# A two-layer float32 streaming-encoder trunk: reordered first feed-forward products, a kept transpose, and squared ReLU two tiles at a time

## The chip, the core and the metric

The kernel runs on one core of one Trainium2 chip. The metric is the device time of one execution in microseconds (us); a kernel's time is the median of several executions.

## What is computed

The input is x of 256 frames by 2048 features (batch 1), float32 throughout. The reference, cut to its skeleton:

```python
# layer 1 ("mixer A")
u = rms_norm(h, a_norm_g);  q, k, v, fz = split(u @ a_w_in)      # 16 heads of 128
q = rms_norm(q) ; k = rms_norm(k)                                # per head
logf = log_sigmoid(fz + a_b_f)
o = softmax(q k^T / sqrt(128) + c_q - c_k, causal) v             # c = cumsum(logf)
h = h + o @ a_w_out
h = h + sq_relu_mlp(h, mlp_norm_g[0], mlp_w1[0], mlp_w2[0])
# keys and values for layer 2, once
k_sh, v_sh = split(rms_norm(h, kv_norm_g) @ kv_w);  k_sh = rms_norm(k_sh)
# layer 2 ("mixer B")
q = rms_norm(rms_norm(h, b_norm_g) @ b_w_q)
o = chunked attention of q against k_sh, v_sh with a relative-position bias
h = h + o @ b_w_out
h = h + sq_relu_mlp(h, mlp_norm_g[1], mlp_w1[1], mlp_w2[1])

def sq_relu_mlp(h, g, w1, w2):          # w1: 2048 x 8192, w2: 8192 x 2048
    a = relu(rms_norm(h, g) @ w1)
    return (a * a) @ w2
```

## The kernel before, in words

**Precision by splitting.** A float32 number is held as a high part in TensorE's float32r type and a low part, the rest. A weight unit (128 partitions x 1024 numbers, 512 KB) is brought by one DMA into `raw` (4 buffers), cast to `hi` on ACT (L99), and `lo = raw - hi` is formed on DVE (L100); `hi` and `lo` have 3 buffers each. `fetch()` keeps two units ready ahead of the one in use. Activations are split in the same way: an activation tile `act` has the high part of 256 frames in its first 256 columns and the low part in the other 256. Of the four cross products only high x high, high x low and low x high are computed.

**Two kinds of panel.** `panel_a` has the activations as stationary operand and streams 512 weight columns: for each of 16 input tiles and 2 blocks of frames it issues three 512-column products (L222, L223, L224). A panel is 96 products over 8 weight units. `panel_b`, used for the first feed-forward product alone, has the weights as stationary operand and streams the activations, so that its output is already transposed for the second product. It makes two output tiles of 128 features at a time; for each of 16 input tiles and each output tile it issues one product of the high weights with both halves of x (512 columns, L238) and one of the low weights with the high half (256 columns, L239). A unit holds 4 input tiles, so 8 such pairs, and a panel has 4 units.

**The feed-forward block** (`mlp`) runs over four chunks of 2048 hidden features. A chunk is 8 `panel_b` panels, whose outputs go through `act` (sum of the two halves, squared ReLU, split: ACT L447 and L452, DVE L448, L450 and L453), and then four `panel_a` panels that multiply the chunk by its part of the second weight matrix and add to the residual `h` (L269, L271). The residual is kept with frames on the partitions.

**Turning the residual.** The next product needs the residual transposed. After each of a block's last panels, `next_x` puts two calls of `turn_x` into `fill`, a list of small jobs; `run_fill` takes one entry after each weight unit. `turn_x` transposes two feature tiles (four transposes of 128x128 on TensorE, L132) into the single PSUM buffer of the pool `ps_t`, and `split_x` reads them out with the gain (ACT L123, DVE L124). The same buffer serves `turn`, which transposes normed heads (`qn`, L254) for queries and keys (L261, read by ACT L262), and a few others. The head norm in front of it goes ACT (L246), DVE (L248, L250), POOL (L252), DVE (L254).

After layer 1's feed-forward block the residual is transposed twice: once with the gain of layer 2's queries (`xb`, from `next_x`), and once more for the shared keys and values (`xkv`), with the order of frames reversed inside each block of 128. The second set of 8 `turn_x` calls is put into `fill` and runs during the four panels of the queries (about 1130 to 1230 us), one call every second unit.

**Buffers and order.** PSUM accumulators come from `ps_acc`, 4 buffers of one bank, and activation tiles from `acts`, 32 buffers. The framework that compiles the kernel sets all waits and may move instructions of one engine past each other, by its own reckoning of when their inputs and buffers are there; what it has set is then fixed, and every engine runs its list in order.

Of the kernel before, what the change touches and what calls it, by code (L numbers as in the profile page):

```python
# [21 lines left out]
GH = 4  # L22
# [8 lines left out]
UB = UN // 256  # L31
# [4 lines left out]
def trunk(ctx: ExitStack, tc: tile.TileContext, xT, xr, gs, hg, bf, wgate, w_in, w_oa, w1a, w2a,  # L36
          w_kv, w_qb, w_ob, w1b, w2b, rel, out):
    nc = tc.nc
    V, S, G, TE = nc.vector, nc.scalar, nc.gpsimd, nc.tensor

    def pool(name, bufs, **kw):
        return ctx.enter_context(tc.tile_pool(name=name, bufs=bufs, **kw))

    PSUM = bass.MemoryType.PSUM
    wsp = pool("wsp", 3)
    acts = pool("acts", 32)
    wraw = pool("wraw", 4)
# [11 lines left out]
    h = [const.tile([P, D], F32, name=f"h{b}") for b in range(NB)]  # L59
# [23 lines left out]
    for srcs in ((w_in,), (w_oa,), (w1a, w2a), (w_qb,), (w_kv,), (w_ob,), (w1b, w2b)):  # L83
        n = srcs[0].shape[0] // (NCH if len(srcs) > 1 else 1)
# [25 lines left out]
    def run_fill():  # L110
        if fill:
            for f in fill.popleft():
                f()

    def blocks(t, flipped=False):
        t = t.rearrange("p (b t) -> p b t", b=NB)
        return t[:, :, ::-1] if flipped else t

    def split_x(src, m, which, flipped=False):
        g = gsb[:, which * KT + m : which * KT + m + 1]  # L120
        x = acts.tile([P, 2 * T], F32R, name="act")
        src = blocks(src, flipped)
        S.activation(blocks(x[:, :T]), src, AF.Copy, scale=g)  # L123
        V.scalar_tensor_tensor(blocks(x[:, T:]), src, g, blocks(x[:, :T].bitcast(F32)), op0=ALU.mult, op1=ALU.subtract)  # L124
        return x

    def turn_x(k0, which, into, flipped=False):
        pt = ps_t.tile([P, 512], F32, name="pt")
        for j in range(2):
            for b in range(NB):  # L130
                c = (k0 + j) * P
                TE.transpose(pt[:, j * T + b * P : j * T + (b + 1) * P], h[b][:, c : c + P], ident)  # L132
        for j in range(2):
            into.append(split_x(pt[:, j * T : (j + 1) * T], k0 + j, which, flipped))

    class ColumnStats:
        def __init__(self):
# [70 lines left out]
            self.flipped = f  # L208

    def panel_a(x, evac, before=None):  # L210
        ps = [ps_acc.tile([P, 512], F32, name="acc") for _ in range(NB)]
        for u in range(KT // UA):
            if before:
                before(u)
            hi, lo = fetch(min(u, AHEAD) if before else AHEAD)
            for j in range(UA):
                k = u * UA + j
                wh, wl = hi[:, j * 512 : (j + 1) * 512], lo[:, j * 512 : (j + 1) * 512]
                for b in range(NB):
                    xh = x[k][:, b * P : (b + 1) * P]  # L220
                    xl = x[k][:, T + b * P : T + (b + 1) * P]
                    TE.matmul(ps[b], xh, wh, start=k == 0, stop=False)  # L222
                    TE.matmul(ps[b], xh, wl, start=False, stop=False)  # L223
                    TE.matmul(ps[b], xl, wh, start=False, stop=k == KT - 1)  # L224
            run_fill()
        for b in range(NB):
            evac(b, ps[b])

    def panel_b(x, evac, n):
        for m in range(n):  # L230
            ps = [ps_acc.tile([P, 512], F32, name="acc") for _ in range(2)]
            for u in range(KT // UB):
                hi, lo = fetch()
                for i in range(2):
                    for j in range(UB):
                        k = u * UB + j
                        c = j * 256 + i * P
                        TE.matmul(ps[i], hi[:, c : c + P], x[k], start=k == 0, stop=False)  # L238
                        TE.matmul(ps[i][:, :T], lo[:, c : c + P], x[k][:, :T], start=False, stop=k == KT - 1)  # L239
                run_fill()  # L240
            for i in range(2):
                evac(2 * m + i, ps[i])

    def head_norm(ps, e, gcol, dst, b):
        sq = wk.tile([P, 512], F32, name="sq", tag="wk")
# [28 lines left out]
    def next_x(n, r2, stats, which, into):  # L274
        add_h = residual(n, r2)

        def f(b, ps):
            add_h(b, ps)
            stats.add(b, n)
            if b == NB - 1:  # L280
                add_fill([[lambda j=j: turn_x(4 * n + 2 * j, which, into)] for j in range(2)])
        return f

    def softmax(st, g, a, q, k, bias, cq):
# [28 lines left out]
    def values(st, a, v, o, i):  # L313
        po = ps_o.tile([P, 512], F32, name="po")
        TE.matmul(po[:, :T], v[:, 0, a * P : (a + 1) * P], st["pT"][:, :T], start=True, stop=False)  # L315
        TE.matmul(po[:, P:T], v[:, 1, a * P : (a + 1) * P], st["pT"][:, T:], start=False, stop=True)  # L316
        o[i] = acts.tile([P, 2 * T], F32R, name="act")
# [27 lines left out]
    x = []  # L345
# [80 lines left out]
    o = [None] * H  # L426
    for g in range(NG):
        q, k, v = qkv.tile([P, GH, T], F32, name="q", bufs=4), qkv_tile("k"), qkv.tile([P, NB, 512], F32, name="v")
# [12 lines left out]
    def mlp(x, st, last):  # L441
        for c in range(NCH):
            hid = []

            def act(m, ps):
                tb = wk.tile([P, T], F32, name="tb", tag="wk")
                S.activation(tb, ps[:, T:], AF.Copy)  # L447
                V.tensor_tensor(tb, ps[:, :T], tb, op=ALU.add)  # L448
                a = wk.tile([P, T], F32, name="a", tag="wk")
                V.scalar_tensor_tensor(a, tb, 0.0, tb, op0=ALU.max, op1=ALU.mult)  # L450
                t = acts.tile([P, 2 * T], F32R, name="act")
                S.activation(t[:, :T], a, AF.Copy)  # L452
                V.tensor_tensor(t[:, T:], a, t[:, :T].bitcast(F32), op=ALU.subtract)  # L453
                hid.append(t)

            panel_b(x, act, 8)
# [8 lines left out]
    mlp(x1, st1, lambda n, r2: next_x(n, r2, st2, 3, xb))  # L465
# [19 lines left out]
    o = [None] * H  # L485
    for g in range(NG):
        k, v = qkv_tile("k"), qkv.tile([P, NB, 512], F32, name="v")
# [80 lines left out]
```

## Time and profile before

| | |
|---|---|
| median of 3 runs | 2231.23 us (2229.55 to 2231.32) |
| the profiled execution, its own time | 2231.47 us |
| its span | 2229.7 us |
| TensorE (PE) | busy 2216.1 us, 99% |
| weight loads (PEld) | busy 1860.5 us, 83% |
| VectorE (DVE) / ScalarE (ACT) | 1294.5 us (58%) / 1053.5 us (47%) |
| DMA | 416.24 MB, mean 187 GB/s |
| 512-column product, `panel_a` (L222, L223, L224) | 2048 each; 397, 390, 390 ns |
| 512-column product, `panel_b` (L238) | 2048; 397 ns |
| 256-column product, `panel_b` (L239) | 2048; 281 ns |
| transposes in `turn_x` (L132) | 128; 275 ns |

Times in a row of the profile are the recorded duration of one instruction. Products on TensorE are pipelined, so that one starts before the recorded end of the one ahead; what a product costs in a stream is the distance from its start to the next start. In a timeline row the first number is the start from the beginning of the span, the second the duration (both in us), then engine, line, operation, output tile, input tiles and shape; in square brackets stands the idle time before it and what ended it. A row of a table of stretches gives the stretch, its length, the busy time and number of instructions of PE, PEld, DVE, ACT and POOL, the granted TensorE clock (1.00 is full), the DMA share and GB/s.

### The profile page before, as it was taken

What the parts mean: (1) busy time and instruction counts of PE and PEld (TensorE: products, weight loads), DVE (VectorE), ACT (ScalarE), POOL (GpSimd) and SP (SyncE); (2) the same over time, 40 slices, a digit from 0 to 9 for tenths busy, and PEclk for the clock granted to TensorE, in tenths of its full rate; (3) what the DMA queues carried; (4) which work ended last, traced back from release to release, by engine and by line L of the source; (5) the groups of instructions that cost most, each with busy time, mean ns of one, the idle gap of its engine ahead of it and who ended that gap; (6) DMA issues with size and microseconds to landing.
All of it is one profiled execution on the core that took longest, in us unless ns stands there. A gap on an engine that the chain in (4) does not pass through costs nothing.

```text
span 2229.7 us, 28337 instructions
## 1 busy us (share of the span) xinstructions
PE 2216.1 (99%) x10894; PEld 1860.5 (83%) x10894; DVE 1294.5 (58%) x1726; ACT 1053.5 (47%) x1451; POOL 41.6 (2%) x48
## 2 busy tenths in 40 slices
PE   9999999999999999999999999999999999999999
PEld 7788888888888888888887888888888888888887
DVE  6665555665565565565555655656655655655654
ACT  5554555543444444344455555555434444443443
POOL 1000000000000000000001000000000000000000
PEclk9999999999999999999999999999999999999999
DMA  7655556566656666666555655556666666666665
GB/s 260 201 173 173 183 175 186 183 190 194 192 184 194 189 189 189 193 186 189 181 181 163 184 176 163 166 183 185 189 193 190 188 191 192 187 192 193 187 200 162
DMA packets 117943, 416.24 MB, mean 187 GB/s; under 512 B 13216, under 2 KB 17456, under 8 KB 117552
## 3 DMA queue, kind: packets, MB, share of 16 engines
q1 hardware_dynamic: 117808, 414.44, 60.2%
q8 instruction: 85, 1.39, 0.3%
q14 instruction: 50, 0.41, 0.0%
HBM read 412.26 MB, written 2.12 MB: 186 GB/s over the span
## 4 chain that ended last, share of the span: by engine, by line
PE 96%; DMA 1%; DVE 1%; issue 0%; POOL 0%; ACT 0%; SPq 0%; DVEq 0%; ACTq 0%; POOLq 0%
PE acc L238 21%; PE acc L224 20%; PE acc L222 20%; PE acc L223 20%; PE acc L239 11%; DMA raw<-in_w_in 1%; PE pt L132 1%; PE pt L261 1%; PE po L315 1%; PE s L287 1%; DMA bias<-cd 1%; PE pt L309 0%; POOL rn L252 0%; DVE lo L100 0%; PE po L316 0%
## 5 line engine op out<-in xcount | busy, mean ns | idle before, releaser
L100 DVE TENSOR_TENSOR lo<-raw,hi 128x1024 fp32r<-128x1024 f32 (+1 forms) x770 | 938.9, 1221 | 809.9 <-ACT hi L99 809.7
L99 ACT ACTIVATE hi<-raw 128x1024 fp32r<-128x1024 f32 (+1 forms) x770 | 815.0, 1058 | 1054.3 <-PE acc L224 623.9
L222 PE MATMUL acc<-hi,act 128*128 128x512 f32 x2048 | 812.6, 397 | 2.1 <-ACT act L123 1.3
L224 PE MATMUL acc<-hi,act 128*128 128x512 f32 x2048 | 798.8, 390 | 0.5 <-DVE act L124 0.5
L223 PE MATMUL acc<-lo,act 128*128 128x512 f32 x2048 | 798.4, 390 | 0.1
L238 PE MATMUL acc<-act,hi 128*128 128x512 f32 x2048 | 721.1, 397 | 0.0
L239 PE MATMUL acc<-act,lo 128*128 128x256 f32 x2048 | 574.9, 281 | 0.0
L238 PEld LDWEIGHTS acc<-act,hi 128*128 128x128 f32 x2048 | 384.4, 188 | 93.0
L224 PEld LDWEIGHTS acc<-hi,act 128*128 128x128 f32 x2048 | 384.6, 188 | 83.0 <-DVE act L124 1.6
L222 PEld LDWEIGHTS acc<-hi,act 128*128 128x128 f32 x2048 | 384.9, 188 | 79.6 <-ACT act L123 2.0
L223 PEld LDWEIGHTS acc<-lo,act 128*128 128x128 f32 x2048 | 385.2, 188 | 77.8 <-DVE lo L100 1.6
L239 PEld LDWEIGHTS acc<-act,lo 128*128 128x128 f32 x2048 | 386.9, 189 | 0.3
L447 ACT ACTIVATE tb<-acc 128x256 f32<-128x256 f32 x128 | 47.9, 374 | 26.9 <-PE acc L239 26.9
L450 DVE SCALAR_TENSOR_TENSOR a<-tb 128x256 f32<-128x256 f32 x128 | 54.4, 425 | 4.4
L453 DVE TENSOR_TENSOR act<-a,act 128x256 fp32r<-128x256 f32 x128 | 53.5, 418 | 0.0
L448 DVE TENSOR_TENSOR tb<-acc,tb 128x256 f32<-128x256 f32 x128 | 53.4, 417 | 0.0
L452 ACT ACTIVATE act<-a 128x256 fp32r<-128x256 f32 x128 | 51.2, 400 | 0.0
L123 ACT ACTIVATE act<-pt,gsb 128x256 fp32r<-128x256 f32 x64 | 30.0, 469 | 38.0 <-DVE act L124 33.6
L252 POOL TENSOR_TENSOR rn<-vv,mhalf 128x4 f32<-128x4 f32 x32 | 36.0, 1125 | 407.0 <-DVE vv L250 407.0
L254 DVE TENSOR_TENSOR qn<-acc,rn 128x512 f32<-128x512 f32 x32 | 22.1, 691 | 35.7 <-POOL rn L252 35.7
L124 DVE SCALAR_TENSOR_TENSOR act<-pt,gsb,act 128x256 fp32r<-128x256 f32 x64 | 30.7, 480 | 16.7 <-ACT act L123 16.7
L300 ACT ACTIVATE pr<-t,nm 128x128 f32<-128x128 f32 x64 | 28.7, 449 | 14.8 <-DVE nm L299 14.4
(107 smaller groups left out, 551.0 us busy)
## 6 DMA issues: line engine op xcount, KB each, us to landing
raw<-in_w1a SPq DMA_DIRECT2D x128, 512.0 KB, 3.8
raw<-in_w2a SPq DMA_DIRECT2D x128, 512.0 KB, 3.7
raw<-in_w1b SPq DMA_DIRECT2D x128, 512.0 KB, 4.2
raw<-in_w2b SPq DMA_DIRECT2D x128, 512.0 KB, 4.3
raw<-in_w_in SPq DMA_DIRECT2D x94, 512.0 KB, 3.9
raw<-in_w_kv SPq DMA_DIRECT2D x64, 512.0 KB, 3.6
raw<-in_w_oa SPq DMA_DIRECT2D x32, 512.0 KB, 3.6
raw<-in_w_qb SPq DMA_DIRECT2D x32, 512.0 KB, 3.6
```

Of the source, the lines that this page charges most:

```text
L99: S.activation(hi[:, c], raw[:, c], AF.Copy)
L100: V.tensor_tensor(lo[:, c], raw[:, c], hi[:, c].bitcast(F32), op=ALU.subtract)
L222: TE.matmul(ps[b], xh, wh, start=k == 0, stop=False)
L223: TE.matmul(ps[b], xh, wl, start=False, stop=False)
L224: TE.matmul(ps[b], xl, wh, start=False, stop=k == KT - 1)
L238: TE.matmul(ps[i], hi[:, c : c + P], x[k], start=k == 0, stop=False)
L239: TE.matmul(ps[i][:, :T], lo[:, c : c + P], x[k][:, :T], start=False, stop=k == KT - 1)
L447: S.activation(tb, ps[:, T:], AF.Copy)
L448: V.tensor_tensor(tb, ps[:, :T], tb, op=ALU.add)
L450: V.scalar_tensor_tensor(a, tb, 0.0, tb, op0=ALU.max, op1=ALU.mult)
L452: S.activation(t[:, :T], a, AF.Copy)
L453: V.tensor_tensor(t[:, T:], a, t[:, :T].bitcast(F32), op=ALU.subtract)
```

## The change

1. *Order of the first products.* `panel_b` takes a function that lists the 16 products of a weight unit as (part, q): part 0 is the 512-column product, part 1 the 256-column one, and q = 0..7 counts output tile and input tile. The orders, with W for a 512-column product and N for a 256-column one: `pairs` WN WN ..., as before; `later` NW NW ..., except that in a panel's first unit each output tile begins with its W; `split` WW NN WW NN ...; `mirror` WN NW WN NW ...; `grouped` eight W, then eight N. Layer 1's four chunks use: pairs; later; grouped in the chunk's first unit and pairs after it; split in the first unit and pairs after it. Layer 2's use: split; mirror; grouped; later in the first unit and pairs after it.
2. *Transposed residual kept.* The `turn_x` calls that make `xb` also copy the transposed residual out of PSUM, before any gain, with one 512-column ACT copy each, into four tiles that use the buffers of `k` and `v` of the `qkv` pool. The splits for `xkv` read these tiles (with the frames reversed) instead of transposing again: 32 transposes are gone, and the number of splits is the same.
3. *Two output tiles at once.* The two accumulators of a panel are one PSUM tile of two banks (`ps_acc`: 2 buffers instead of 4), and activation tiles come in pairs (`acts`: 16 buffers of twice the size). `act` works on both output tiles in one instruction each: ACT copy, DVE sum, ACT ReLU in place, ACT square, ACT square into float32r, DVE difference.

```diff
-    acts = pool("acts", 32)
+    acts = pool("acts", 16)
-    ps_acc = pool("ps_acc", 4, space=PSUM)
+    ps_acc = pool("ps_acc", 2, space=PSUM)
...
+    def acc_pair():
+        t = ps_acc.tile([P, 2 * 512], F32, name="acc")
+        return t, [t[:, i * 512 : (i + 1) * 512] for i in range(2)]
+    part = [None]
+    def half(m):
+        if m % 2 == 0:
+            part[0] = acts.tile([P, 2, 2 * T], F32R, name="act")
+        return part[0][:, m % 2, :]
...
-    def turn_x(k0, which, into, flipped=False):
+    def turn_x(k0, which, into, keep=None):
...
-            into.append(split_x(pt[:, j * T : (j + 1) * T], k0 + j, which, flipped))
+            into.append(split_x(pt[:, j * T : (j + 1) * T], k0 + j, which))
+        if keep is not None:
+            if k0 % GH == 0:
+                keep.append(qkv.tile([P, GH, T], F32, name="kv"[k0 // (2 * GH)]))
+            S.activation(keep[-1][:, k0 % GH : k0 % GH + 2, :], pt.rearrange("p (j t) -> p j t", j=2), AF.Copy)
...
+    NQ = 2 * UB
+    def pairs(u):
+        return [(p, q) for q in range(NQ) for p in (0, 1)]
+    def later(u):
+        return [(p, q) for q in range(NQ) for p in ((0, 1) if u == 0 and q % UB == 0 else (1, 0))]
+    def split(u):
+        return [(p, q + i) for q in range(0, NQ, 2) for p in (0, 1) for i in (0, 1)]
+    def mirror(u):
+        return [pq for q in range(0, NQ, 2) for pq in ((0, q), (1, q), (1, q + 1), (0, q + 1))]
+    def grouped(u):
+        return [(p, q) for p in (0, 1) for q in range(NQ)]
+    def order(first, rest):
+        return lambda m, u: (first if m == 0 and u == 0 else rest)(u)
+    def panel_b(x, evac, n, of):
...
+                for n_, (part, q) in enumerate(todo):
+                    i, j = divmod(q, UB)
...
+                    if part == 0:
+                        TE.matmul(ps[i], hi[:, c : c + P], x[k], start=k == 0, stop=last)
+                    else:
+                        TE.matmul(ps[i][:, :T], lo[:, c : c + P], x[k][:, :T], start=False, stop=last)
...
-            def act(m, ps):
-                tb = wk.tile([P, T], F32, name="tb", tag="wk")
-                S.activation(tb, ps[:, T:], AF.Copy)
-                V.tensor_tensor(tb, ps[:, :T], tb, op=ALU.add)
-                a = wk.tile([P, T], F32, name="a", tag="wk")
-                V.scalar_tensor_tensor(a, tb, 0.0, tb, op0=ALU.max, op1=ALU.mult)
-                t = acts.tile([P, 2 * T], F32R, name="act")
-                S.activation(t[:, :T], a, AF.Copy)
-                V.tensor_tensor(t[:, T:], a, t[:, :T].bitcast(F32), op=ALU.subtract)
-                hid.append(t)
+            def act(ps):
+                z = wk.tile([P, 2, T], F32, name="z", tag="wk")
+                S.activation(z, ps[:, :, 1, :], AF.Copy)
+                V.tensor_tensor(z, ps[:, :, 0, :], z, op=ALU.add)
+                S.activation(z, z, AF.Relu)
+                a = wk.tile([P, 2, T], F32, name="a", tag="wk")
+                S.activation(a, z, AF.Square)
+                t = acts.tile([P, 2, 2 * T], F32R, name="act")
+                S.activation(t[:, :, :T], z, AF.Square)
+                V.tensor_tensor(t[:, :, T:], a, t[:, :, :T].bitcast(F32), op=ALU.subtract)
+                hid.extend(t[:, i, :] for i in range(2))
...
+    mlp(x1, st1, lambda n, r2: next_x(n, r2, st2, 3, xb, hT),
+        (order(pairs, pairs), order(later, later), order(grouped, pairs), order(split, pairs)))
...
+    def again(k):
+        for m in (k, k + 1):
+            xkv.append(split_x(hT[m // GH][:, m % GH, :], m, 2, True))
-    add_fill([[], [], [st2.both], [st2.flip]] + [[] for _ in range(6)] + [it for k in range(0, KT, 2) for it in ([lambda k=k: turn_x(k, 2, xkv, True)], [])])
+    add_fill([[], [], [st2.both], [st2.flip]] + [[] for _ in range(6)] + [it for k in range(0, KT, 2) for it in ([lambda k=k: again(k)], [])])
...
-    mlp(x3, st3, store)
+    mlp(x3, st3, store, (order(split, split), order(mirror, mirror), order(grouped, grouped), order(later, pairs)))
```

More of the change, by code (lines that the diff above doesn't have):

```diff
@@ L117, in blocks @@
         return t[:, :, ::-1] if flipped else t
+    def acc_pair():
[6 more added lines that the diff above has]
+        return part[0][:, m % 2, :]
     def split_x(src, m, which, flipped=False):
         g = gsb[:, which * KT + m : which * KT + m + 1]
-        x = acts.tile([P, 2 * T], F32R, name="act")
+        x = half(m)
         src = blocks(src, flipped)
@@ L210, in panel_a @@
     def panel_a(x, evac, before=None):
-        ps = [ps_acc.tile([P, 512], F32, name="acc") for _ in range(NB)]
+        ps = acc_pair()[1]
         for u in range(KT // UA):
@@ L227, in panel_a @@
             evac(b, ps[b])
-    def panel_b(x, evac, n):
+    NQ = 2 * UB
[12 more added lines that the diff above has]
+    def panel_b(x, evac, n, of):
         for m in range(n):
-            ps = [ps_acc.tile([P, 512], F32, name="acc") for _ in range(2)]
+            t, ps = acc_pair()
             for u in range(KT // UB):
                 hi, lo = fetch()
[L234 to L239, printed above, removed]
+                todo = of(m, u)
+                ends = {q // UB: n for n, (_, q) in enumerate(todo)}
+                for n_, (part, q) in enumerate(todo):
+                    i, j = divmod(q, UB)
+                    last = u == KT // UB - 1 and ends[i] == n_
+                    k = u * UB + j
+                    c = j * 256 + i * P
+                    if part == 0:
+                        TE.matmul(ps[i], hi[:, c : c + P], x[k], start=k == 0, stop=last)
+                    else:
+                        TE.matmul(ps[i][:, :T], lo[:, c : c + P], x[k][:, :T], start=False, stop=last)
                 run_fill()
-            for i in range(2):
-                evac(2 * m + i, ps[i])
+            evac(t.rearrange("p (i h t) -> p i h t", i=2, h=2))
     def head_norm(ps, e, gcol, dst, b):
@@ L272, in residual, with next_x @@
         return f
-    def next_x(n, r2, stats, which, into):
+    def next_x(n, r2, stats, which, into, keep=None):
         add_h = residual(n, r2)
@@ L280, in f @@
             if b == NB - 1:
-                add_fill([[lambda j=j: turn_x(4 * n + 2 * j, which, into)] for j in range(2)])
+                add_fill([[lambda j=j: turn_x(4 * n + 2 * j, which, into, keep)] for j in range(2)])
         return f
@@ L316, in values @@
         TE.matmul(po[:, P:T], v[:, 1, a * P : (a + 1) * P], st["pT"][:, T:], start=False, stop=True)
-        o[i] = acts.tile([P, 2 * T], F32R, name="act")
+        o[i] = half(i)
         S.activation(o[i][:, :T], po[:, :T], AF.Copy)
@@ L439, in trunk, with mlp @@
         panel_a(x, v_evac(v, st0.r))
-    def mlp(x, st, last):
+    def mlp(x, st, last, orders):
         for c in range(NCH):
             hid = []
-            def act(m, ps):
-                tb = wk.tile([P, T], F32, name="tb", tag="wk")
-                S.activation(tb, ps[:, T:], AF.Copy)
-                V.tensor_tensor(tb, ps[:, :T], tb, op=ALU.add)
-                a = wk.tile([P, T], F32, name="a", tag="wk")
-                V.scalar_tensor_tensor(a, tb, 0.0, tb, op0=ALU.max, op1=ALU.mult)
-                t = acts.tile([P, 2 * T], F32R, name="act")
-                S.activation(t[:, :T], a, AF.Copy)
-                V.tensor_tensor(t[:, T:], a, t[:, :T].bitcast(F32), op=ALU.subtract)
-                hid.append(t)
-            panel_b(x, act, 8)
+            def act(ps):
[9 more added lines that the diff above has]
+                hid.extend(t[:, i, :] for i in range(2))
+            panel_b(x, act, 8, orders[c])
             for n in range(NG):
@@ L464, in trunk @@
     st2, xb = RowStats("b"), []
-    mlp(x1, st1, lambda n, r2: next_x(n, r2, st2, 3, xb))
+    hT = []
+    mlp(x1, st1, lambda n, r2: next_x(n, r2, st2, 3, xb, hT),
+        (order(pairs, pairs), order(later, later), order(grouped, pairs), order(split, pairs)))
     xkv = []
-    add_fill([[], [], [st2.both], [st2.flip]] + [[] for _ in range(6)] + [it for k in range(0, KT, 2) for it in ([lambda k=k: turn_x(k, 2, xkv, True)], [])])
+    def again(k):
+        for m in (k, k + 1):
+            xkv.append(split_x(hT[m // GH][:, m % GH, :], m, 2, True))
+    add_fill([[], [], [st2.both], [st2.flip]] + [[] for _ in range(6)] + [it for k in range(0, KT, 2) for it in ([lambda k=k: again(k)], [])])
     qs = []
```

## The prediction

> **What bounds the kernel now.** I read the page first (busy shares, then the chain that ended last), then the timeline of TensorE inside the first feed-forward products, then the table of stretches by chunk, then the timeline of the layer-2 query panels, where the kernel turns the residual for the keys and values.
>
> ```profile
> PE 2216.1 (99%) x10894; PEld 1860.5 (83%) x10894; DVE 1294.5 (58%) x1726; ACT 1053.5 (47%) x1451; POOL 41.6 (2%) x48
> PE 96%; DMA 1%; DVE 1%; issue 0%; POOL 0%; ACT 0%; SPq 0%; DVEq 0%; ACTq 0%; POOLq 0%
> PE acc L238 21%; PE acc L224 20%; PE acc L222 20%; PE acc L223 20%; PE acc L239 11%; DMA raw<-in_w_in 1%; PE pt L132 1%; PE pt L261 1%; PE po L315 1%; PE s L287 1%; DMA bias<-cd 1%; PE pt L309 0%; POOL rn L252 0%; DVE lo L100 0%; PE po L316
> ```
>
> TensorE is the bound: 96% of the chain, and DVE (58%) and ACT (47%) only matter where TensorE waits for them. So the change is worth what it takes from TensorE's instruction stream, from the distances between its products, or from its few waits. Recorded durations overlap (a 512-column product shows 0.39 us, and the next starts earlier), so I count distances between starts. L238 is the wide product (512 columns: weight high part by both halves of x), L239 the narrow one (256 columns: weight low part by the high half).
>
> ```profile
> 440.22 0.39 PE L238 MATMUL acc<-act,hi 128*128 128x512 f32 x1
> 440.22 0.19 PEld L239 LDWEIGHTS acc<-act,lo 128*128 128x128 f32 x1
> 440.45 0.28 PE L239 MATMUL acc<-act,lo 128*128 128x256 f32 x1
> 440.45 0.19 PEld L238 LDWEIGHTS acc<-act,hi 128*128 128x128 f32 x1
> 440.57 0.39 PE L238 MATMUL acc<-act,hi 128*128 128x512 f32 x1
> ```
>
> ```profile
> 600.03 0.40 PE L238 MATMUL acc<-act,hi 128*128 128x512 f32 x1
> 600.26 0.28 PE L239 MATMUL acc<-act,lo 128*128 128x256 f32 x1
> 600.38 0.40 PE L238 MATMUL acc<-act,hi 128*128 128x512 f32 x1
> 600.61 0.28 PE L239 MATMUL acc<-act,lo 128*128 128x256 f32 x1
> 600.73 0.40 PE L238 MATMUL acc<-act,hi 128*128 128x512 f32 x1
> 600.97 0.28 PE L239 MATMUL acc<-act,lo 128*128 128x256 f32 x1
> 601.09 0.40 PE L238 MATMUL acc<-act,hi 128*128 128x512 f32 x1
> ```
>
> The next weights start loading with the product ahead, so the load is hidden. But the same pair runs at two speeds. In layer 1's first chunk (440 us) it takes 230 + 116.5 = 346.5 ns, steadily. In the second (600 us) three pairs take 1.06 us, 353.3 ns each, in a cycle that the starts in the trace show to the nanosecond: 233+117, 241+120, 236+113. The table of stretches, one row per chunk of first products, shows which chunks are which:
>
> ```profile
> 408.19:498.11 89.92, 89.91 (x521) 79.07 (x520) 58.09 (x84) 46.20 (x69) 0.00 (x0) 1.00 0.61 188
> 585.20:675.63 90.43, 90.43 (x513) 78.47 (x512) 55.98 (x78) 43.18 (x61) 0.00 (x0) 1.00 0.60 187
> ```
>
> 256 pairs at 353.3 ns are 90.44 us, which all chunks show but the first of each layer. Those take 89.92 although they also hold 8 transposes: they start in the slow cycle and leave it when transposes fall between a wide and a narrow product, so that the narrow one comes first afterwards. The fast speed is worth 256 x 6.8 ns = 1.74 us a chunk. The clock is 1.00 in both.
>
> **The change part by part.** Profiled run: 2231.47 us for a span of 2229.7 (1.8 us around it); the median of the three runs is 2231.23, 0.24 less.
>
> (1) Transposes for keys and values, removed: 8 calls of four.
>
> ```profile
> 1166.12 0.44 PE pt L132 x4
> 1177.79 0.39 PE L222 MATMUL acc<-hi,act 128*128 128x512 f32 x1
> 1178.45 0.47 DVE L124 SCALAR_TENSOR_TENSOR act<-pt,gsb,act 128x256 fp32r<-128x256 f32 x1
> 1179.07 0.63 PE L261 MATMUL pt<-ident,qn 128*128 128x128 f32 x4 [0.89 <-DVE act L124]
> ```
>
> Each four take 0.44 us of TensorE, nothing beside them: 8 x 0.44 = 3.5 us. And they hold the one ps_t buffer. The row at 1179.07 is the head norm's transpose waiting for that buffer, until DVE's L124 has read it; L124 was queued on DVE behind the qn product (L254), which waits for POOL. From the product at 1177.79 it is 1.28 us where 0.227 is usual: 1.05 lost, again at 1203.56 (1.27), and 0.27 more at 1157.00. Without turn_x there, the buffer is free: 2.1 + 0.3 = 2.4 us. The splits themselves stay (ACT L123 0.47, DVE L124 0.48, 16 of each) and read SBUF. Next late could be the head norm's own POOL chain; layer 1's query panels have it without turn_x and show no such wait. Sum of (1): -5.9 us, bounds -6.2 and -3.5.
>
> (2) The copy kept of the transposed residual, added: 8 ACT copies of 128x512 out of PSUM. Nearest row: L262 (q<-pt, same shape), 0.68 us. ACT has room, but the copy also holds ps_t, and TensorE's next transposes wait for that:
>
> ```profile
> 1058.62 1.06 ACT L99 ACTIVATE hi<-raw 128x1024 fp32r<-128x1024 f32 x1
> 1058.67 0.48 DVE L124 SCALAR_TENSOR_TENSOR act<-pt,gsb,act 128x256 fp32r<-128x256 f32 x1 [0.55 <-ACT act L123]
> ```
>
> L124 ends at 1059.15, and the next four transposes start at once after it, some 0.25 us late already. This is so for the second turn_x behind each of the four last panels. The copy comes behind L124 and perhaps behind the cast at 1058.62 (ends 1059.68, then 0.68): the buffer is free at 1060.4, 1.2 us later. Upper bound 4 x 1.2 = 4.9 us; lower bound 0, as the transposes stand 16 products behind the first four where a unit has 12: whoever ordered the program already places them by the expected release, and can place them 4 products further. I take the low side, +0.5 us. Queued behind such a wait are the panel's products.
>
> (3) The order of first products. "pairs" is today's. "later" puts the narrow first, with the same alternation. "split" and "mirror" turn half the alternations into wide-wide and narrow-narrow: 128 of each in a chunk; "grouped" 7 of 8: 224. Wide-wide is known from the second products, 227 ns. Narrow-narrow is nowhere in the trace. Its nearest rows: a narrow product ahead of a wide one, 113 to 120 ns, with a load behind it just the same; I take the median, 117. A pair is then 344 ns against 353.3 in layer 2's chunks 2 and 3 (mirror, grouped): 9.3 x (128 + 224) = 3.3 us; against 346.5 in its first (split): 2.5 x 128 = 0.3. With 113 it is 5.5 together, with 120 it is 2.2.
>
> (4) The cycle. The other changed chunks (layer 1's second, "later"; its third and fourth and layer 2's fourth, where only the first unit is reordered) keep the alternation but enter it differently. In the trace one disturbance of two led into the fast speed, the one with the narrow product first. I count two of the four chunks freed: -3.5 us; bounds -7.0, and +3.5 if the two fast chunks are lost instead.
>
> (5) Everything else, 0. Two output tiles at once: DVE goes from 6 x 0.42 to 2 x 0.69 us, ACT from 4 x 0.39 to one copy and three passes over 512 elements (L262 0.68, L184 0.62), 2.5 us of the 11.3 that a panel lasts, beside four casts (4.2). The output is read one panel later (hid 14 and 15 in the last unit, 19 us on). If the cover went: a cast L99 that stood behind copy, add and three passes would come 3.4 us late; a weight unit has 5.6 us from the buffer's release to its use, cast and low part need 2.3, so only then does it start to show. PSUM tiles in pairs are written again a panel (11 us) later, activations in pairs are freed one product later, the first panel waits for weight DMA (5.5 us at 4.0) more than for x.
>
> Sum: -5.9 + 0.5 - 3.6 - 3.5 = -12.5, so a span of 2217.2, a time of 2219.0.
>
> **The rivals.** *Order is worth nothing* (0.20): if each product's distance is its own, only (1) and (2) are left, -5.4: 2226. For it: both speeds come with the same order. Against: 227 ns between wide products, below both 230 and 241. The Trainium skill (TensorE: Matmul & The Clock Gate, "The mechanism") has weight loads overlap running products only when the row groups differ, and all loads here use all 128 rows; by that rule order would indeed be worth nothing. The rows at 440.22 and 440.45, where load and product start together, disagree with it.
>
> *All four chunks are freed, and narrow-narrow takes 113 ns* (0.14): -5.9 + 0.5 - 5.5 - 7.0 = -17.9: 2213.
>
> *The copy takes back the gain* (0.07): 4.9 from the ps_t waits and nothing from order: -1.0, 2230.
>
> *Slower: the load behind a narrow product shows* (0.08). LDWEIGHTS is recorded at 188 ns, a narrow product streams for 113; wide products hide it, and after a narrow one it may be loading two ahead that hides it today. If narrow-narrow costs 188, the 480 of them lose 61.7 x 352 + 68.5 x 128 ns = 30.5 us, against 5.4 won: 2256. It decides from about 137 ns on (126 is break-even for order alone, 5.4 us over 480 adds 11). Against: the load for the wide product starts with the narrow one ahead (440.45) and the wide one starts 0.12 us later, so 188 is latency, not rate. The Trainium skill (same page, "LDWEIGHTS") gives columns over 1.2, 107 ns for 128 columns, an estimate that would fit behind a narrow product.
>
> The forecast has 0.51.
>
> **How the numbers follow.** A measurement of this kernel can tell 0.2%, 4.5 us. The forecast and the all-freed case are faster (0.65); of 2226, some 5 under the median, 0.14 of 0.20 counts as faster and 0.06 as the same; 2230 is the same (0.06), 0.01 beyond. Faster 0.79, same 0.12, slower 0.09. The range takes in 2213 with 2 us of unknown sizes below, and the high end of the copy's price above: 2211 to 2230.
>
> **What would show it.** Right: 96 transposes at L132's place; no wait of L261's transposes for the splits; a chunk row of about 90.4 falling to 88.7 where the alternation is freed, and to some 89.2 (mirror) and 88.4 (grouped); (1)'s stretch 1130 to 1230 shorter by some 6 us. Wrong: narrow-narrow starts beyond 126 ns apart; waits for the kept copy at the transposes near 1060, 1083, 1106 and 1128; casts that TensorE waits for in the first products.

## The result, and the profile after

The changed kernel takes 2217.74 us, median of 3 runs (2217.04 to 2218.31), against 2231.23 before; the ratio is 0.9942, interval 0.9919 to 0.9964. Run again on one chip beside nine executions of the kernel before, it took 2219.05 against 2229.12 us, 10.1 us less by the medians; the ratio was 0.9954 (0.9941 to 0.9966). Why the two gains differ is part of what follows.

The page of the changed kernel, parts 1 and 4. In its line numbers L277 and L279 are the wide and the narrow first product (L238 and L239 before), L237 to L239 the second products, L143 the transposes of `turn_x`, L134 and L135 the splits on ACT and DVE, L149 the kept copy, L462 the mask addition to the bias, L354 the values product and L358 the DVE instruction that frees its buffer.

```profile
PE 2206.1 (100%) x10862; PEld 1854.1 (84%) x10862; DVE 1240.8 (56%) x1470; ACT 1110.7 (50%) x1459; POOL 52.4 (2%) x48
PE 97%; DMA 1%; DVE 1%; issue 0%; ACT 0%; SPq 0%; POOL 0%; DVEq 0%; ACTq 0%
PE acc L277 21%; PE acc L239 20%; PE acc L237 20%; PE acc L238 20%; PE acc L279 11%; PE s L326 1%; PE po L354 1%; PE pt L300 1%; PE pt L143 1%; DMA raw<-in_w_in 0%; PE pt L348 0%; PE s L325 0%; PE po L355 0%; DMA bias<-cd 0%; ACT hi L99 0%
```

TensorE is the bound as before: 32 instructions fewer, 10.0 us less busy, the span 13.9 us shorter (2229.7 to 2215.8). Cutting both traces at the same places gives where that lies: layer 1's attention stage -3.6 us, the eight chunks of first products -3.8, the stretch from layer 1's last four feed-forward panels to layer 2's first feed-forward product (the middle stretch below) -7.1, and the end behind the last product +0.7; all else is under 0.1.

The chunks, one row each of the table of stretches of the changed kernel: layer 1's second (later) and fourth (split in the first unit, then pairs), layer 2's first (split), second (mirror) and third (grouped).

```profile
581.64:671.99 90.35, 90.35 (x514) 78.47 (x513) 50.23 (x48) 48.27 (x60) 0.00 (x0) 1.00 0.61 187
936.47:1025.22 88.75, 88.75 (x513) 77.60 (x512) 49.58 (x48) 49.02 (x60) 0.00 (x0) 1.00 0.63 191
1503.55:1593.84 90.29, 90.26 (x522) 78.58 (x521) 51.63 (x55) 52.08 (x69) 0.00 (x0) 1.00 0.62 187
1680.90:1770.07 89.17, 89.17 (x513) 77.81 (x512) 50.23 (x48) 48.26 (x60) 0.00 (x0) 1.00 0.62 189
1857.12:1946.48 89.36, 89.36 (x514) 78.66 (x513) 49.59 (x48) 49.88 (x61) 0.00 (x0) 1.00 0.63 190
```

One chunk of the four with the alternation fell into the fast cycle (88.75; the third and the last stayed at 90.40 and 90.42). Mirror and grouped won 1.27 and 1.08 us against 90.44, split lost 0.37 against the 89.92 of before. In the timeline of the grouped chunk, eight wide products take 1.84 us from the first one's start to the start of the narrow ones, 230 ns each, and the eight narrow ones 0.95 us, 119 ns each:

```profile
1859.88 2.00 PE L277 MATMUL acc<-act,hi 128*128 128x512 f32 x8
1861.72 1.11 PE L279 MATMUL acc<-act,lo 128*128 128x256 f32 x8
1862.67 1.55 PE L277 MATMUL acc<-act,hi 128*128 128x512 f32 x6
```

The second to fourth query panels, which held the second set of transposes, before and after:

```profile
1144.70:1219.20 74.50, 72.62 (x346) 59.27 (x345) 44.57 (x58) 38.97 (x53) 9.79 (x6) 1.00 0.55 170
```

```profile
1138.40:1206.60 68.20, 68.20 (x314) 56.22 (x313) 38.23 (x42) 32.18 (x36) 8.86 (x6) 1.00 0.64 185
```

TensorE has 32 instructions fewer (x346, x314). Of the 6.3 us, 1.9 are idle time that is gone (74.50 less 72.62), the rest is busy time: 3.5 for the transposes, and some 0.9 of waiting that lay under the recorded end of the product ahead.

The second call of `turn_x` behind one of layer 1's last panels, timeline, before and in the changed kernel:

```profile
1058.83 0.39 PE L224 MATMUL acc<-hi,act 128*128 128x512 f32 x1
1059.30 0.63 PE L132 MATMUL pt<-ident,h 128*128 128x128 f32 x4
```

```profile
1053.22 0.48 DVE L135 SCALAR_TENSOR_TENSOR act<-pt,gsb,act 128x256 fp32r<-128x256 f32 x1 [0.54 <-ACT act L134]
1054.12 0.58 ACT L149 ACTIVATE k<-pt 128x512 f32<-128x512 f32 x1
1054.76 0.66 PE L143 MATMUL pt<-ident,h 128*128 128x128 f32 x4
```

The kept copy does stand behind the cast and end last, at 1054.70, and the transposes follow at once. But the wait costs less than before: 0.26 us from the last product's start (1054.50) to the first transpose, where it was 0.47 (1058.83 to 1059.30); 0.23 is usual between products.

What the prediction had not looked at is layer 1's attention stage. The timelines of DVE, TensorE and SP there, before:

```profile
101.56 1.29 DVE L423 TENSOR_TENSOR bias<-bias,tri 128x512 f32<-128x512 f32 x2 [3.14 <-DMA bias<-cd]
103.91 0.42 DVE L319 TENSOR_TENSOR act<-po,act 128x256 fp32r<-128x256 f32 x1
...
104.38 1.21 PE L315 MATMUL po<-prT,v 128*128 128x256 f32 x2 [2.41 <-DVE act L319]
...
95.00 0.33 SPq L421 DMA_DIRECT2D bias<-cd  x1
```

and after:

```profile
99.28 1.29 DVE L462 TENSOR_TENSOR bias<-bias,tri 128x512 f32<-128x512 f32 x2 [1.18 <-DMA bias<-cd]
101.62 0.42 DVE L358 TENSOR_TENSOR act<-po,act 128x256 fp32r<-128x256 f32 x1
...
102.71 0.38 PE L354 MATMUL po<-prT,v 128*128 128x256 f32 x1
...
93.42 0.33 SPq L460 DMA_DIRECT2D bias<-cd  x1
```

The DMA in the last row brings the bias of the third head group, while the first group's attention is still running. It goes into the buffer that the first group's softmax frees: the last addition of the first group's bias ends at 94.98 us before and at 93.39 after, and the DMA is issued at once. It takes 6.5 us to land. DVE has the mask addition to this bias in its list ahead of the instruction that frees the values buffer, so that DVE stands for 3.14 us and TensorE for 2.41. In the trace of before, TensorE's granted clock (the 0.50 in this row) is then halved for 3.4 us:

```profile
104.43:107.85 3.42, 3.42 (x9) 2.85 (x10) 1.45 (x2) 0.38 (x1) 0.00 (x0) 0.50 0.64 186
```

After, the DMA is issued 1.6 us earlier, and the panel with the wait starts 0.9 us later (85.46 against 84.54), so that the DMA is issued 8.0 us behind the panel's start instead of 10.5, and TensorE does not wait.

### The profile page after: what moved, and what is told of

The parts are those of the page before. It is cut to its first block, busy times and chain, and to the rows that moved or that the text cites. A ratio compares the mean times of both kernels' runs of the same rounds, so it can differ in the third digit from the quotient of the medians.

```text
span 2215.8 us, 28102 instructions
## 1 busy us (share of the span) xinstructions
PE 2206.1 (100%) x10862; PEld 1854.1 (84%) x10862; DVE 1240.8 (56%) x1470; ACT 1110.7 (50%) x1459; POOL 52.4 (2%) x48
## 4 chain that ended last, share of the span: by engine, by line
PE 97%; DMA 1%; DVE 1%; issue 0%; ACT 0%; SPq 0%; POOL 0%; DVEq 0%; ACTq 0%
PE acc L277 21%; PE acc L239 20%; PE acc L237 20%; PE acc L238 20%; PE acc L279 11%; PE s L326 1%; PE po L354 1%; PE pt L300 1%; PE pt L143 1%; DMA raw<-in_w_in 0%; PE pt L348 0%; PE s L325 0%; PE po L355 0%; DMA bias<-cd 0%; ACT hi L99 0%
## 5 line engine op out<-in xcount | busy, mean ns | idle before, releaser
L237 PE MATMUL acc<-hi,act 128*128 128x512 f32 x2048 | 811.6, 396 | 0.7 <-ACT act L134 0.7
L239 PE MATMUL acc<-hi,act 128*128 128x512 f32 x2048 | 799.6, 390 | 1.3 <-DVE act L135 1.2
L238 PE MATMUL acc<-lo,act 128*128 128x512 f32 x2048 | 797.7, 390 | 0.6 <-DVE lo L100 0.6
L277 PE MATMUL acc<-act,hi 128*128 128x512 f32 x2048 | 672.1, 395 | 0.0
L279 PE MATMUL acc<-act,lo 128*128 128x256 f32 x2048 | 490.1, 280 | 0.0
L239 PEld LDWEIGHTS acc<-hi,act 128*128 128x128 f32 x2048 | 384.4, 188 | 83.9 <-DVE act L135 2.8
L238 PEld LDWEIGHTS acc<-lo,act 128*128 128x128 f32 x2048 | 385.0, 188 | 78.7 <-DVE lo L100 1.9
L237 PEld LDWEIGHTS acc<-hi,act 128*128 128x128 f32 x2048 | 384.9, 188 | 77.6 <-ACT act L134 1.4
L277 PEld LDWEIGHTS acc<-act,hi 128*128 128x128 f32 x2048 | 363.1, 188 | 64.1
L279 PEld LDWEIGHTS acc<-act,lo 128*128 128x128 f32 x2048 | 372.1, 189 | 27.2
L493 DVE TENSOR_TENSOR act<-a,act 128x512 fp32r<-128x512 f32 x64 | 44.3, 693 | 31.6 <-ACT act L492 31.6
L487 DVE TENSOR_TENSOR z<-acc,z 128x512 f32<-128x512 f32 x64 | 43.9, 686 | 18.0 <-ACT z L486 18.0
L486 ACT ACTIVATE z<-acc 128x512 f32<-128x512 f32 x64 | 37.5, 585 | 28.0 <-PE acc L277 28.0
L490 ACT ACTIVATE a<-z 128x512 f32<-128x512 f32 x64 | 40.5, 633 | 2.0
L488 ACT ACTIVATE z<-z 128x512 f32<-128x512 f32 x64 | 39.4, 616 | 2.8 <-DVE z L487 2.8
L492 ACT ACTIVATE act<-z 128x512 fp32r<-128x512 f32 x64 | 39.4, 616 | 0.0
L285 ACT ACTIVATE sq<-acc 128x512 f32<-128x512 f32 x32 | 19.1, 598 | 36.6 <-PE acc L239 26.9
L134 ACT ACTIVATE act<-pt,gsb 128x256 fp32r<-128x256 f32 x48 | 22.5, 469 | 28.6 <-DVE act L135 23.3
```

The lines of the kernel that those rows point to most:

```text
L487: V.tensor_tensor(z, ps[:, :, 0, :], z, op=ALU.add)
L488: S.activation(z, z, AF.Relu)
L490: S.activation(a, z, AF.Square)
L493: V.tensor_tensor(t[:, :, T:], a, t[:, :, :T].bitcast(F32), op=ALU.subtract)
```

## Experiments

**Each edit alone, and the wait in the attention stage.** Four kernels made from the kernel before, on one chip with it; there the kernel before had a median of 2228.62 us in 28 executions (2226.19 to 2230.90).

The kept transpose alone (edit abridged, comments added):

```diff
+    mlp(x1, st1, lambda n, r2: next_x(n, r2, st2, 3, xb, hT))    # turn_x copies pt into hT
...
-    [lambda k=k: turn_x(k, 2, xkv, True)]
+    [lambda k=k: again(k)]                                        # splits read hT
```

> The kept transposed residual alone; order of products, accumulators and squared ReLU as before. Theory A (each edit acts in its own stage, as the two traces suggest): 7.1 us less, all of it between the end of layer 1's feed-forward block and the end of layer 2's query panels, about 0.8 of it in the four last feed-forward panels and 6.3 in the four query panels; layer 1's attention stage stays at 402.8 us from its first product; some 2224 us. Rival B, the prediction's own terms: 5.9 us won in the query panels and 0.5 lost in the four last panels to the kept copy, 2226 us. Rival C: the 3.6 us that the attention stage lost between the two traces also come from this edit, through the program order: 2220 us.

2222.85 us, ratio 0.9972 (0.9961 to 0.9983), 5.8 us by the medians. In its profile the middle stretch takes 478.7 us against 485.5, 6.8 less: the second to fourth query panels 22.7 each where they took 24.5, 25.8 and 24.3 (6.3 won), the three panels ahead of the queries 0.2 less each, the first query panel the same to 0.1. The attention stage (401.0) still holds the wait for the values buffer (2.1 us), and the bias DMAs have kept their places in SP's list, so rival C is out; the gain in the last panels puts B's 0.5 us of loss out too.

The order of the first products alone (L238 and L239 of before, in the orders of the change):

> The order of the first products alone, eight chunks as in the change; accumulators, squared ReLU and transposes as before. Theory A: the chunks take what they take in the changed kernel (89.9, 90.35, 90.4, 88.75; 90.3, 89.2, 89.4, 90.4 us), 3.8 us less than before in sum: 2227.5 us. Rival B, the prediction's terms: 7.1 us less, 2224 us. Rival C: the chunks' times came from the paired accumulators and not from the order; then they stay at 89.9 and 90.44 and the time at 2231.

2225.84 us, 0.9988 (0.9979 to 0.9997). The chunks take 89.92, 90.35, 90.40, 88.75, 90.29, 89.17, 89.36 and 90.42 us: the changed kernel's to 0.01, 3.8 us in sum. So the order alone makes them. The time moved 2.8 us, nearer to theory A's 3.8 than to B's 7.1, and its range is wide (2223.5 to 2230.3): the profiled execution, the slowest of ten, waited 3.8 us for the values buffer at one place.

The mask on POOL:

```diff
-            V.tensor_tensor(nb[:, :, c], nb[:, :, c], tri.unsqueeze(1).to_broadcast([P, GH, P]), op=ALU.add)
+            G.tensor_tensor(nb[:, :, c], nb[:, :, c], tri.unsqueeze(1).to_broadcast([P, GH, P]), op=ALU.add)
```

> The kernel before, with one edit: the causal mask is added to the decay bias on POOL instead of DVE. Theory A (TensorE's wait for the values buffer at about 104 us is DVE held by the mask addition, which waits for the bias DMA, with the reader of the values buffer queued behind it; the idle time then halves the TensorE clock for 3.4 us): the wait and the slow stretch go, the attention stage is 3.5 to 4.3 us shorter, some 2227.5 us. Rival: the reader of the values buffer is late for another reason (the cast on ACT, the transposes of the probabilities): under 1 us, 2230.5 to 2231 us.

2225.80 us, 0.9988 (0.9978 to 0.9997); the attention stage took 398.1 us, 4.7 less than in the profile of before, and TensorE's list of waits has no values buffer any more. The panel with the wait, before and in this kernel:

```profile
84.40:116.20 31.80, 29.39 (x135) 24.18 (x134) 21.35 (x45) 16.21 (x35) 0.00 (x0) 0.95 0.54 169
```

```profile
85.40:112.90 27.50, 27.50 (x135) 22.98 (x134) 19.71 (x38) 15.25 (x32) 4.96 (x4) 1.00 0.61 185
```

Both hold the same products; 4.3 us less, and the mean clock goes from 0.95 to 1.00. Ten executions of this kernel lie within 1.4 us, 28 of the kernel before within 4.7. So the wait is the mask addition's. The time fell by 2.8 us, less than the profiles' 4.7, so the wait differs from one execution to the next.

Accumulators in pairs alone (edit abridged; `panel_b` has the same):

```diff
-    ps_acc = pool("ps_acc", 4, space=PSUM)
+    ps_acc = pool("ps_acc", 2, space=PSUM)
-        ps = [ps_acc.tile([P, 512], F32, name="acc") for _ in range(NB)]
+        ps = acc_pair()[1]
```

> The kernel before, with one edit: accumulators allocated two at a time (2 buffers of two PSUM banks instead of 4 of one). Theory A: this edit alone moves the issue of the second bias DMA ahead of two weight DMAs, and with it the attention stage falls by 3.6 us as between the two traces; nothing else moves: 2227.6 us. Rival: the attention stage moved by the wider squared ReLU or by the paired activation tiles; then this kernel stays within 0.5 us of before, or is slower where a pair is held until both halves are read.

In the profile the attention stage fell as expected, the time did not: 2229.89 us, 1.0008 (0.9998 to 1.0018). The attention stage took 398.8 us, with 0.5 us of waiting for the values buffer. The step behind it differs from theory A's: it is the first of the four bias DMAs that stands two weight DMAs earlier in SP's list (behind 26 instead of 28); the second and third keep their places (behind 29 and 34). The program order of the first group's softmax shifts with it, so the buffer for the third DMA comes free sooner. That DMA is issued 8.0 to 8.1 us behind the start of the panel with the wait in every profile with paired accumulators, and 10.2 to 10.8 in the three without them that have the mask on DVE; TensorE's wait there is at most 0.5 us in the first kind and 2.1 to 3.8 in the second. But the query panels took 1.0 us more (two waits for the transpose buffer, 2.8 us together instead of 1.8), and the end 0.7 us more. The end can be read in DVE's last instructions, before and in the changed kernel:

```profile
2225.17 1.43 DVE L271 SCALAR_TENSOR_TENSOR h<-acc,qn,h 128x512 f32<-128x512 f32 x2 [5.16 <-PE acc L224]
```

```profile
2211.27 1.41 DVE L310 SCALAR_TENSOR_TENSOR h<-acc,qn,h 128x512 f32<-128x512 f32 x2 [5.84 <-PE acc L239]
```

The last products start at 2225.42 and 2210.84. With single accumulators the first block's sum starts before the second block's last product; with the pair it waits for the whole tile, 0.43 us behind. Every kernel here with paired accumulators has 5.0 us behind the last product's start, every one without them 4.2 to 4.3. The query panels and the end together lose 1.7 us, and this kernel's median is 1.3 us above that of the kernel before. That leaves the attention stage a gain of 0.4 us, at most 2.1 by the interval: the 4.0 us between the two profiles are not what a typical execution gains.

Two tiles at once alone (paired accumulators, paired activations, squared ReLU over 512 elements):

> The paired accumulators, the paired activation tiles and the squared ReLU over two output tiles alone; order of products and transposes for keys and values as before. Theory A (the squared ReLU lies beside the products, and the pairing only moves instructions in the attention and query stages): chunks at 89.92 and 90.44 us as before, the query panels with the waits for the transpose buffer as before or 1 us more, layer 1's attention stage 398.5 to 402 us: 2226 to 2231 us. Rival: the longer chain on ACT (copy, ReLU, two squares) makes casts late, and chunks take over 90.6 us.

One execution: 2230.29 us, beside one of the kernel before at 2227.27; chunks at 89.92 and 90.44 exactly as before, attention stage 399.7, middle stretch 486.5, the last two as with the accumulators alone (398.8 and 486.5). The wider squared ReLU costs TensorE nothing in the first products.

**The changed kernel again, and one order everywhere.** Four to five executions each on one chip, the kernel before at 2229.12 us there (nine executions).

> The changed kernel unaltered, beside the kernel before on one chip. Theory A: the kernel before loses between 0 and some 5 us in layer 1's attention stage, differently in each execution (its mask addition on DVE waits for the bias DMA), so that the 13.5 us of the two medians is 11 us of lasting gain (7.1 from the kept transpose, 3.8 from the order) and the rest chance; the ratio comes out at 0.995 (11 us) against a median of the kernel before near 2228.6. Rival: the paired accumulators take 3.6 us out of the attention stage for good: 0.9935 to 0.9942 (13 to 14.5 us).

2219.05 us, 0.9954 (0.9941 to 0.9966): near theory A's figure; the interval goes from 7.6 to 13.2 us, so it excludes most of the rival's 13 to 14.5. In the profiled execution the attention stage took 402.0 us: the panel with the mask's wait took 27.5 us as in the first profile, but this time TensorE waited 2.1 us for an activation in the first panel and again ran at half clock for 3.4 us. The stage as a whole varies with or without the change.

```diff
-        (order(pairs, pairs), order(later, later), order(grouped, pairs), order(split, pairs)))
+        (order(pairs, pairs),) + (order(split, pairs),) * 3)
-    mlp(x3, st3, store, (order(split, split), order(mirror, mirror), order(grouped, grouped), order(later, pairs)))
+    mlp(x3, st3, store, (order(pairs, pairs),) + (order(split, pairs),) * 3)
```

> The changed kernel with one order everywhere: in each layer the first chunk in pairs, the other three with split in their first unit and pairs after it, as only layer 1's fourth chunk has it in the changed kernel. Theory A (the first unit chooses which of two lasting cycles the alternation falls into, and the split unit chooses the 346.5 ns one wherever it stands): six chunks of 88.75 us and two of 89.92, 6.3 us less than the changed kernel in sum. Rival: the fast chunk was due to its place (what ran before it, the buffers it has); then the other five stay between 90.3 and 90.44, and the kernel loses what mirror and grouped had won, 2.4 us more than the changed kernel.

2211.46 us, 0.9918 (0.9905 to 0.9932) against before, 7.6 us under the changed kernel by the medians. All six chunks take 88.75 us and the first of each layer 89.92; 6.3 us in sum, as expected; the further 1.3 us by the medians lie outside the chunks. The place of a chunk has nothing to do with it; the first 16 products have. This version beats both kernels.

> The kernel with split first units, and the causal mask added on POOL besides. Theory A: the chunks as in that kernel, and the attention stage at 398.1 us as when the mask alone was moved, with executions within 1.5 us of each other: 1 us less than with the split first units alone, some 2210.5 us. Rival: with paired accumulators the bias DMA is already early enough, and moving the mask wins nothing: the same time as with the split first units alone.

2211.24 us (2210.48 to 2212.19), no different. In the profiles the attention stage is 2.2 us shorter (398.3 against 400.5), the times do not show it: with four and five executions this stays inconclusive.

**What chooses the cycle.** W is a wide product, N a narrow one; after what is listed, the alternation runs through the rest of the chunk.

> The changed kernel with the alternation in all chunks (W wide, N narrow) and only the beginning of a chunk's first unit differing: layer 1: pairs; WNNW four times; WWNN once; WNNW once; layer 2: pairs; WWWNNN once; WWNN twice; pairs. Theory A (what counts is the distance of the last narrow product before the alternation begins: in the changed kernel a group that ended with 120 ns was followed by the slow cycle, one that ended with 112 ns by the fast one, and the second WWNN ends with 112): WWNN twice gives 88.75 us; WWNN once, WWWNNN and pairs give 90.4; the two with WNNW are open. Rival B: any group of narrow products with as many wide ones ahead frees the chunk: WWNN once and WWWNNN give 88.75 too. Rival C: it takes the whole unit: WWNN twice stays at 90.4.

One execution, 2220.14 us. The table of stretches of this kernel; in order WNNW four times, WWNN once, WWWNNN once, WWNN twice:

```profile
581.78:672.18 90.40, 90.40 (x514) 78.38 (x513) 49.57 (x48) 49.06 (x60) 0.00 (x0) 1.00 0.61 187
759.28:849.72 90.44, 90.44 (x514) 78.48 (x513) 49.58 (x48) 49.05 (x60) 0.00 (x0) 1.00 0.62 187
1682.62:1773.04 90.42, 90.42 (x513) 78.39 (x512) 49.57 (x48) 49.06 (x60) 0.00 (x0) 1.00 0.62 186
1860.14:1948.88 88.74, 88.74 (x513) 77.61 (x512) 49.56 (x48) 49.02 (x60) 0.00 (x0) 1.00 0.64 191
```

Eight products, WWNN twice, are enough to win 1.7 us over the 252 pairs that follow; rivals B and C are out. One WNNW stayed slow too (90.43).

> As in the kernel with different beginnings, the alternation everywhere and only a chunk's first products differing: layer 1: pairs; WWNN three times; WWNN twice; WN and then WWNN twice; layer 2: pairs; WWWWNNNN twice; WWNN three times; WWNN twice. Theory A (the narrow product just ahead of the alternation decides: 112 ns leads to the fast cycle, 119 or 120 to the slow one; in layer 1's fourth chunk of the changed kernel the groups ended with 120, 112, 119 and 112): three times gives 90.4 us in both places, twice 88.75 in both, WWWWNNNN twice 90.4 (its narrow run ends with 120); WN ahead of two groups is open. Rival: the number of wide-wide pairs, or of products out of the alternation, decides, from two groups on: then three times is fast too.

One execution, 2216.66 us. The rows of WWNN three times (layer 1) and of WWWWNNNN twice:

```profile
581.67:672.08 90.41, 90.41 (x513) 78.52 (x512) 49.59 (x48) 49.03 (x60) 0.00 (x0) 1.00 0.60 187
1680.82:1769.58 88.76, 88.76 (x513) 78.36 (x512) 49.58 (x48) 49.08 (x60) 0.00 (x0) 1.00 0.62 190
```

WWNN three times gave 90.41 in both places, twice 88.74 in both, so the number of groups as such is not it, and the outcome repeats. WN ahead of two groups gave 90.42. But WWWWNNNN twice gave 88.76, against theory A; its last narrow product stood at 117 ns and not at the 120 that theory A took from the grouped chunk. Nor does a short last distance decide: WNNW four times ends its narrow products with 112 ns and stayed slow, and plain pairs begin with 113 or 114 ns and end in the slow cycle. Where nothing disturbs a chunk, its first products choose its cycle, reproducibly, and each cycle then lasts; the rule by which they choose stays open.

## Why the prediction was right, point by point

The time, 2217.7 against 2219.0 forecast, lies well inside the range, and the direction holds in both comparisons. It came so close by luck, because misses on both sides cancelled: between the two profiles, the five terms missed by -0.4, -1.3, +1.6, +1.7 and -2.9 us.

- **(1) Transposes removed: right.** -5.9 forecast, -6.3 measured in the second to fourth query panels. Both parts are there: the transposes (3.5), and the head norm's waits for ps_t (2.8 against the 2.4 forecast). The POOL chain, named as next late, did not show.
- **(2) The kept copy: wrong sign.** +0.5 forecast, -0.8 measured over the four panels behind the last four sums, 0.2 in each. The placement shifted as argued (15 products lay between the two sets of four transposes, not the 16 of the forecast, and 20 after), and fitted better than I allowed: the copy ends at 1054.70, just when the next instruction is due, while before the transposes stood 0.25 us early for L124's end. I had taken the old misfit as a floor.
- **(3) Wide-wide and narrow-narrow: mis-sized.** -3.6 forecast, -2.0 measured (split +0.37, mirror -1.27, grouped -1.08). The narrow was priced well: 115 ns in split and mirror, 119 in grouped, against 117. The wide-wide was not: 227 was taken from panels where every neighbour is wide, and next to narrow products it measured 234, 233 and 230.5. The effect reaches over several products: behind eight narrow ones, the wide ones in the grouped chunk stand 233, 236, 228, 233 and 231 ns apart, and only then 226 to 227. Split is the case where this turned the sign. Mirror came out as forecast (89.17 for some 89.2) by luck: its wide-wide and narrow-narrow pair took 347.6 ns instead of 344, and the alternations left in it, which I had kept at 353.3, took 349.0. The break-even of 126 ns for narrow-narrow leaves out the split chunk; over all 480 it is 124.5, which changes nothing at 115 to 119.
- **(4) The cycle: two speeds, but not the rule.** Two of four chunks freed were forecast, one was; -1.8 instead of -3.5. The count was one of two disturbances in the trace, and the reason for it, that the narrow product comes first, fell: the two chunks that use `later` stayed at 90.35 and 90.42, and the one that was freed begins with two wide products. That one of the four came free was luck. The bound of +3.5 was too wide: of the two fast chunks, layer 1's keeps its order, and layer 2's is priced in (3).
- **(5) Everything else at nothing: wrong in two places.** The paired accumulators changed the program order in the attention stage, so that the third bias DMA is issued sooner, and the stage fell by 3.6 us in the profiled execution; and they lengthened the end by 0.7. I had put the whole program order outside the edited stages down as unchanged.
- **What lasts.** -7.1 - 3.8 + 0.7 = -10.2 us, near the 10.1 by the medians of the second comparison, whose interval goes from 7.6 to 13.2. The further 3 us of the first comparison fit the attention stage, where its two profiles differ by 3.6; that the kernel before lost more there in those three runs than it does in others is inferred from its times (2231.23 against 2228.62 and 2229.12), not shown. How much of the attention stage's gain lasts stays open.

Of the rivals, "order is worth nothing" fell with the second kernel: the order alone makes the chunks' 3.8 us. "The copy takes back the gain" fell with the first. The slower one, narrow-narrow at 188 ns, fell in the changed kernel's trace: of the seven distances in a run of eight, the first is 113 or 114 ns and the others 119 to 120, nothing near 188. "All four freed", with narrow-narrow at 113 ns, fell too: one chunk was freed, and narrow-narrow took 115 to 119.

## What to carry to other kernels

Count a stream of products by the distances between their starts, chunk by chunk: two steady speeds of the same instructions can hide in one mean, and a handful of reordered products at the start can choose the better one. Before an edit to buffers is priced at nothing, ask what it does to the program order elsewhere, and which queue there already stands behind a late DMA. A gain that one profiled execution shows in a stage that waits for DMA should be measured over many executions before it is credited.

## What the runs showed of the hardware

The alternation of a 512- and a 256-column float32r product has two lasting cycles on an undisturbed TensorE at full clock, 346.5 and 353.3 ns a pair. Waits of TensorE of 2.41, 2.08 and 2.13 us (the kernel before, the kept transpose alone, the changed kernel again) were each followed within 1.8 us by 3.4 us at half the granted clock, and so was one of 1.55 us in the first panel of the kernel with the mask on POOL; one of 1.3 us in the first panel of the kernel before was not. In the kernel before, wait and slow stretch cost the panel 4.3 us. The wait of 0.68 us at the end of the kernel, where the sum of one bank of a two-bank accumulator tile waits for the products into the other, is one that the framework has set; no run shows whether the chip needs it.
